# One attention layer on one core: where a last round's adds run, in which order its last pair comes, and when a gate-and-up tile uses its third weights again

## The chip, the cores and the metric

The kernel runs on one core of one Trainium2 chip. A core has TensorE (matrix products, into the eight banks of PSUM), VectorE, ScalarE, GpSimd (POOL on the profile's rows) and SyncE, which here only starts transfers. Each engine works through its own queue in order, and the engines wait for one another on semaphores. The metric is the device time of one execution in microseconds.

## The reference

One decoder layer over 512 tokens of width 1024, in f32: a feed-forward block (SwiGLU) before and one after a mixing block of windowed attention, a convolution module and attention to a memory. The change touches the two feed-forward blocks:

```python
def swiglu(x, w_gate, w_up, w_down):
    return (jax.nn.silu(x @ w_gate) * (x @ w_up)) @ w_down
...
x = x + 0.5 * swiglu(rms_norm(x, g_ffn1[l]), w_ffn1_gate[l], w_ffn1_up[l], w_ffn1_down[l])
...
x = x + 0.5 * swiglu(rms_norm(x, g_ffn2[l]), w_ffn2_gate[l], w_ffn2_up[l], w_ffn2_down[l])
```

The inner width is 2816, that is 22 tiles of 128.

## The kernel before

Everything is held transposed: features on the 128 partitions, tokens along the free dimension, so `x` is eight row blocks of 128 by 512. Precision comes from splitting each operand into a high and a low part (`fp32r`) and making three products for each block: high by high, high by low, low by high. For weights the class `Weights` does this: a load into a raw tile (`wraw`, four buffers, L178 on SyncE), sums of weights where a tile needs them (`make_sums`, L160 to L163, and `four`, L147 to L150, on VectorE), a cast on ScalarE (L214, L208) and the difference on VectorE (L219, L209). The split weights lie in four buffers in turn; one kind lies in a buffer of its own, `vhi` and `vlo`. `W.next()` hands out the next item and asks for the conversion of those three ahead.

**Gate and up tiles.** For most of the 22 tiles (`fast`, 18 in the first block and 19 in the second) gate and up are made together with seven half-width products in place of eight, after Strassen's way with sums of weights and of inputs. `product` issues one of them: twelve matmuls of 256 columns (L609 to L611). A tile has three banks: `b` and `c` of half width and `de` of full width. Its order is: first weights `w0` (B_11 into `b`, copied out by L620; B_21 into the left half of `de`), second `w1` (B_Q1 into the right half of `de`, copied out by L624; B_Q2 on top of `b`, copied out by L626), third `w2` (B_22 on top of the right half of `de`). L629 and L630 make `g` of that. Then comes the first part of a down step, if the tile has one; then `w3` (`vhi`, `vlo`), whose product B_T4 goes into `c` and is copied out by L638; then the second use of `w2`, B_T3, on top of `b`. L640 makes `u` from `c`'s copy and `b`, L644 multiplies it by `g`, and L567 and L568 split the result (`hh`, `hl`). The rest of the down step follows.

**Down steps.** `down` multiplies finished tiles of a round by down weights (`mm3`, L414 to L416) and adds half of the result to `x` (L671). Steps of one round are spread over the tiles of the next: most tiles carry one load with two steps, of 24 matmuls of 256 columns.

**The last round.** In the second block the last four tiles' down products are made in the same seven-product way. `paired` prepares the inputs (L472 to L492, seven blocks for each of two pairs of tiles), and `seven(g)` for g = 0 to 3 makes the row blocks 2g and 2g+1 of the output. `prod` issues six matmuls (L510 to L512). `half` copies a partial sum out with a factor (L515, ScalarE). `add` puts sums that several row blocks share into `x`: for g = 0 and 1 by an accumulating DMA on POOL (L521), for g = 2 and 3 by VectorE (L519). `leave` makes a row block of the output (L529, VectorE) and stores it (L532, SyncE). The leaves of g are put off into `seven(g+1)` by way of the list `later`; only g = 3 leaves its own, first block 6 whole, then the two halves of block 7. Pair g = 2 has the two banks `tp`, the other pairs two of the four banks `mm` each.

**What sets the order.** In the last round the program's own order holds on TensorE, VectorE and ScalarE (`tc.manual_schedule`). Everywhere else a planner in the language's framework orders each engine's queue, by the program's order and by when it reckons operands and buffers to be ready. Buffers and banks are handed on as soon as their last reader is done.

Of the kernel before, what the change touches and what calls it, by code (L numbers as in the profile page):

```python
# [39 lines left out]
T = 512  # L40
# [41 lines left out]
B_T3, B_Q1, B_Q2, B_T4, B_21, B_22, B_11 = range(7)  # L82
H_11, H_21, H_T1, H_T2, H_T4, H_T3, H_22 = range(7)
# [191 lines left out]
def layer(tc, ctx, a):  # L275
# [10 lines left out]
    def nm(s):  # L286
        uid[0] += 1
        return f"{s}_{uid[0]}"

    def mm_bank():  # L290
        return psum.tile([P, T], F32, tag="mm", name=nm("mm"), bufs=4)

    def sc_bank():
        return psum.tile([P, T], F32, tag="sc", name=nm("sc"), bufs=2)
# [4 lines left out]
    def work():  # L299
        return tmp.tile([P, T], F32, tag="t", name=nm("t"), bufs=5)  # L300
# [5 lines left out]
    W = Weights(nc, wpool, dma_ahead=3, conv_ahead=3, bufs=(4, 4))  # L306
# [51 lines left out]
    def atile(name, dtype=F32R):  # L358
        return act.tile([P, T], dtype, tag="h", name=nm(name), bufs=N_ACT)
# [68 lines left out]
    class Norm:  # L428
# [5 lines left out]
        def add(self, d, engine=POOL):  # L434
            sq = work() if d else tmp.tile([P, T], F32, tag="sqsum", name=nm("sqsum"), bufs=1)
            ACT.activation(sq, x[:, d], AF.Square)
            if d == 0:
                self.sum = sq
            else:
                (engine if d < KT - 1 else DVE).tensor_tensor(self.sum, self.sum, sq, op=ALU.add)  # L440
# [20 lines left out]
    def ffn(pool, norm, first, gain, hooks, next_gain, last):  # L461
# [35 lines left out]
        def seven(g):  # L497

            l, r = slice(0, 256), slice(256, 512)
            end = g == 3  # L500
            bank = tp_bank if g == 2 else mm_bank
            b, de, c = bank()[:, l], bank(), sc_bank()[:, l]
            s12, s45 = (kept(), work()) if end else (atile("s12", F32), atile("s45", F32))
            x0, x1 = x[:, 2 * g], x[:, 2 * g + 1]

            def prod(ps, w, at, step, block, first):
                for q in range(2):
                    hi, lo = sevens[q][block]
                    s = slice(at + q * step, at + q * step + P)
                    PE.matmul(ps, w[0][:, s], hi, start=first and q == 0, stop=False, skip_group_check=not first)  # L510
                    PE.matmul(ps, w[0][:, s], lo, start=False, stop=False, skip_group_check=not first)
                    PE.matmul(ps, w[1][:, s], hi, start=False, stop=q == 1, skip_group_check=not first)  # L512

            def half(to, ps, sign=1):
                ACT.activation(to, ps, AF.Copy, scale=0.5 * sign)  # L515

            def add(to, part):
                if g > 1:
                    DVE.tensor_tensor(to, to, part, op=ALU.add)  # L519
                else:  # L520
                    POOL.dma_start(to, part, accum_op=ALU.add)  # L521

            def leave(d, t, ps):
                o = work()[:, : t.stop - t.start]
                xd = x[:, d, t]
                if ps.shape[-1] < t.stop - t.start:
                    o, xd = (v.rearrange("p (a b) -> p a b", a=2) for v in (o, xd))
                    ps = ps.unsqueeze(1).to_broadcast([P, 2, 256])
                DVE.scalar_tensor_tensor(o, ps, 0.5, xd, op0=ALU.mult, op1=ALU.add)  # L529
                if len(o.shape) == 3:  # L530
                    o = o.rearrange("p a b -> p (a b)")
                nc.sync.dma_start(a["out"][d, :, t], o)  # L532

            W.split_to(W.at + 4)
            if g < 2:
                W.four(W.items[W.at + 4][0])
            wa, ws = W.next(), W.next()
            prod(b, wa, 0, 256, H_11, True)
            half(s12[:, l], b)
            prod(de[:, l], wa, 128, 256, H_21, True)  # L540
            prod(de[:, r], ws, 0, 128, H_T1, True)
            half(s45[:, r], de[:, r])
            while later:
                leave(*later.pop(0))
            prod(b, ws, 256, 128, H_T2, False)
            half(s12[:, r], b)
            add(x0, s12)
            prod(c, wa, 512, 128, H_T4, True)
            half(s45[:, l], c, -1)
            add(x1, s45)  # L550
            W.split_to(W.at + 3)
            prod(de[:, r], ws, 768, 128, H_22, False)
            prod(b, ws, 512, 128, H_T3, False)
            whole = slice(0, T)
            if end:
                leave(2 * g, whole, de)
                leave(2 * g + 1, l, b)
                leave(2 * g + 1, r, b)
            else:
                later.extend([(2 * g + 1, whole, b), (2 * g, whole, de)])  # L560

        def hidden(f, t):
            if plan.seven and f >= plan.rounds[-1][0]:
                paired(f, t)
                return
            h_hi[f], h_lo[f] = atile("hh"), atile("hl")
            ACT.copy(h_hi[f], t)  # L567
            DVE.tensor_tensor(h_lo[f], t, h_hi[f].bitcast(F32), op=ALU.subtract)  # L568

        def kept():  # L570
            return pool.tile([P, T], F32, tag="kept", name=nm("kept"), bufs=3)
# [32 lines left out]
        def product(ps, w, woff, block, first):  # L604
            wh, wl = w
            for k in range(4):
                c = slice(woff + k * P, woff + (k + 1) * P)
                one, end = first and k == 0, k == 3
                PE.matmul(ps, wh[:, c], bh[k][:, block], start=one, stop=False, skip_group_check=not first)  # L609
                PE.matmul(ps, wh[:, c], bl[k][:, block], start=False, stop=False, skip_group_check=not first)  # L610
                PE.matmul(ps, wl[:, c], bh[k][:, block], start=False, stop=end, skip_group_check=not first)  # L611

        def fast(f, mid):

            l, r = slice(0, 256), slice(256, 512)
            b, de, c = mm_bank()[:, l], mm_bank(), sc_bank()[:, l]
            s12, s45, g, u = kept(), kept(), work(), work()
            w0 = W.next()
            product(b, w0, 0, B_11, True)
            ACT.copy(s12[:, l], b)  # L620
            product(de[:, l], w0, 512, B_21, True)
            w1 = W.next()
            product(de[:, r], w1, 0, B_Q1, True)
            ACT.activation(s45[:, r], de[:, r], AF.Copy, scale=-1.0)  # L624
            product(b, w1, 512, B_Q2, False)
            ACT.copy(s12[:, r], b)  # L626
            w2 = W.next()
            product(de[:, r], w2, 0, B_22, False)
            DVE.tensor_tensor(g, de, s12, op=ALU.add)  # L629
            ACT.activation(g, g, AF.Silu)  # L630
            rest = []
            for d in mid:
                rest += down(*d)
            if rest:
                rest.pop(0)()
            w3 = W.next()
            product(c, w3, 0, B_T4, True)
            ACT.copy(s45[:, l], c)  # L638
            product(b, w2, 512, B_T3, False)
            DVE.tensor_tensor(  # L640
                u.rearrange("p (a b) -> p a b", a=2), s45.rearrange("p (a b) -> p a b", a=2),
                b.unsqueeze(1).to_broadcast([P, 2, 256]), op=ALU.subtract,
            )
            DVE.tensor_tensor(u, u, g, op=ALU.mult)  # L644
            hidden(f, u)
            for d in rest:
                d()
# [35 lines left out]
        for f in range(NF):  # L683
# [6 lines left out]
            else:  # L690
                g, u = (sc_bank(), sc_bank()) if f % 3 == 2 else (mm_bank(), mm_bank())
# [27 lines left out]
        r = plan.last  # L719
        if plan.seven:  # L720
            W.conv_ahead = -1
            with tc.manual_schedule(engines={mybir.EngineType.PE, mybir.EngineType.DVE, mybir.EngineType.Activation}):
                for g in range(4):
                    seven(g)
            return nxt
# [173 lines left out]
    load, piece, sums, p1, p2 = memory()  # L899
# [6 lines left out]
    with tc.tile_pool(name="fast1", bufs=1) as pool:  # L906
        norm = ffn(pool, norm, STARTS, C_G1, hooks, C_GM, False)
# [4 lines left out]
    with tc.tile_pool(name="fast2", bufs=1) as pool:  # L912
        ffn(pool, norm, [(0, 1, 2, 3, 4, 5, 6), (7,)], C_G2, {}, None, True)
# [490 lines left out]
```

## Time and profile before

| | us |
|---|---|
| runs of the kernel (three) | 861.43, 861.53, 861.96 |
| median | 861.53 |
| the profiled execution | 861.62 |
| its span in the profile | 859.8 |
| TensorE busy in it | 850.1 |
| VectorE busy | 708.9 |
| ScalarE busy | 466.3 |

The span is what the profile covers; the execution's own time has 1.82 us more around it. A row of the timeline gives the start, the duration, engine, line, operation, output and inputs by their names in the program, shapes, how many were merged, and in brackets the idle time before it and what ended that. A row with x2 is two instructions; the next may start a little before the one ahead has ended, so costs within a queue are best taken from start to start. "PE" is TensorE, "DVE" VectorE, "ACT" ScalarE. A waits row gives who waited on whom, then the sum, the number of times and the longest.

### The profile page before, as it was taken

The page shows a single profiled execution, that of the slowest core. Times are in us where ns is not written, and L with a number is a line of the kernel's source. Part 1 is how long each engine was busy: PE and PEld are TensorE (multiplying, and loading weights), DVE is VectorE, ACT ScalarE, POOL GpSimd, SP SyncE. Part 2 cuts the span into 40 slices and gives each one's busy share as a digit, 9 for nine tenths or more (in the row PEclk, how much of TensorE's full clock was granted, in tenths as well). Part 3 has the DMA queues.
Part 4 walks back from the last instruction along what each step waited for, and adds up shares of the span by engine and source line. Part 5 has one row for each costly group of instructions (what it writes and reads, how often), then busy time and mean ns, then how long its engine had stood idle before and what let it go on. Part 6 is the DMA issues. An engine that isn't in the chain of part 4 may idle for free. (4 is left out here: it accounts for less than half of the span.)

```text
span 859.8 us, 15853 instructions
## 1 busy us (share of the span) xinstructions
PE 850.1 (99%) x6397; PEld 788.6 (92%) x6397; DVE 708.9 (82%) x1208; ACT 466.3 (54%) x792; POOL 37.4 (4%) x40
## 2 busy tenths in 40 slices
PE   8999999999999999999999999999999999999997
PEld 5889999999999999988676788889999999999997
DVE  7998977877868897869989985899787878787896
ACT  7465555455654444633948764656554544545554
POOL 0000000000000000300000022120000000000001
PEclk9999999999999999999999999999999999999999
DMA  7335334333453434222010323863334342323325
GB/s 274 123 91 149 105 98 125 98 119 127 129 157 120 123 111 130 74 98 62 13 32 31 113 97 100 178 141 122 123 98 124 99 123 86 114 96 103 95 75 148
DMA packets 36795, 95.13 MB, mean 111 GB/s; under 512 B 3441, under 2 KB 8049, under 8 KB 36721
## 3 DMA queue, kind: packets, MB, share of 16 engines
q1 hardware_dynamic: 32032, 85.99, 32.1%
q0 software_dynamic: 3536, 6.55, 4.6%
q10 hardware_dynamic: 1152, 1.57, 0.6%
q8 instruction: 50, 0.82, 0.4%
q14 instruction: 25, 0.20, 0.1%
HBM read 88.07 MB, written 2.10 MB: 105 GB/s over the span
## 5 line engine op out<-in xcount | busy, mean ns | idle before, releaser
L609 PE MATMUL mm<-bh,w 128*128 128x256 f32 x888 | 245.5, 276 | 0.4 <-ACT kept L624 0.4
L610 PE MATMUL mm<-bl,w 128*128 128x256 f32 x888 | 245.2, 276 | 0.0
L611 PE MATMUL mm<-bh,w 128*128 128x256 f32 x888 | 245.2, 276 | 0.0
L609 PEld LDWEIGHTS mm<-bh,w 128*128 128x128 f32 x888 | 166.7, 188 | 0.8 <-ACT kept L624 0.6
L415 PE MATMUL mm<-hl,w 128*128 128x256 f32 (+1 forms) x584 | 167.3, 287 | 0.0
L416 PE MATMUL mm<-hh,w 128*128 128x256 f32 (+1 forms) x584 | 167.2, 287 | 0.0
L414 PE MATMUL mm<-hh,w 128*128 128x256 f32 (+1 forms) x584 | 167.0, 287 | 0.0
L610 PEld LDWEIGHTS mm<-bl,w 128*128 128x128 f32 x888 | 166.7, 188 | 0.1
L611 PEld LDWEIGHTS mm<-bh,w 128*128 128x128 f32 x888 | 166.7, 188 | 0.0
L214 ACT CAST w<-wraw 128x1024 fp32r<-128x1024 f32 (+2 forms) x119 | 119.1, 1005 | 74.8 <-PE mm L611 23.7
L219 DVE TENSOR_TENSOR w<-wraw,w 128x1024 fp32r<-128x1024 f32 (+2 forms) x113 | 132.5, 1176 | 29.9 <-ACT w L214 26.4
L219 DVE TENSOR_TENSOR w<-s,w 128x1024 fp32r<-128x1024 f32 x78 | 95.3, 1222 | 40.3 <-PE mm L611 34.5
L414 PEld LDWEIGHTS mm<-hh,w 128*128 128x128 f32 x584 | 109.6, 188 | 2.4 <-ACT hh L567 0.3
L415 PEld LDWEIGHTS mm<-hl,w 128*128 128x128 f32 x584 | 109.6, 188 | 2.2
L416 PEld LDWEIGHTS mm<-hh,w 128*128 128x128 f32 x584 | 109.6, 188 | 2.1
L214 ACT CAST w<-s 128x1024 fp32r<-128x1024 f32 x78 | 81.9, 1052 | 27.1 <-PE mm L611 20.4
L414 PE MATMUL mm<-xh,w 128*128 128x512 f32 x176 | 69.7, 401 | 0.5 <-ACT xh L425 0.4
L415 PE MATMUL mm<-xl,w 128*128 128x512 f32 x176 | 69.4, 394 | 0.6 <-DVE xl L426 0.5
L416 PE MATMUL mm<-xh,w 128*128 128x512 f32 x176 | 69.1, 393 | 0.0
L630 ACT ACTIVATE t<-t 128x512 f32<-128x512 f32 x37 | 23.4, 633 | 68.3 <-DVE t L629 68.3
L671 DVE SCALAR_TENSOR_TENSOR x<-mm,x 128x512 f32<-128x512 f32 x80 | 54.2, 683 | 2.0 <-PE mm L416 2.0
L214 ACT CAST vhi<-wraw 128x512 fp32r<-128x512 f32 x37 | 23.0, 621 | 42.7 <-PE sc L610 34.7
(290 smaller groups left out, 1496.8 us busy)
## 6 DMA issues: line engine op xcount, KB each, us to landing
wraw<-in_wgu SPq DMA_DIRECT2D x86, 512.0 KB, 3.6
wraw<-in_wd SPq DMA_DIRECT2D x38, 512.0 KB, 3.6
wraw<-in_win SPq DMA_DIRECT2D x12, 512.0 KB, 3.5
wraw<-in_wd SPq DMA_DIRECT2D x8, 384.0 KB, 3.3
x<-t POOLq DMA_DIRECT2D x8, 256.0 KB, 4.1
out<-t SPq DMA_DIRECT2D x7, 256.0 KB, 2.3
x<-in_xT SPq DMA_DIRECT2D x3, 512.0 KB, 6.8
wraw<-in_wout_a SPq DMA_DIRECT2D x6, 256.0 KB, 2.7
```

What stands on the lines that cost most here:

```text
L214: nc.scalar.copy(hi[:, :cols], raw[:, :cols])
L219: nc.vector.tensor_tensor(lo[:, :cols], raw[:, :cols], hi[:, :cols].bitcast(F32), op=ALU.subtract)
L414: PE.matmul(ps[:, t], wh[:, w], hi(k)[:, t], start=one, stop=False, skip_group_check=cut > 1)
L415: PE.matmul(ps[:, t], wh[:, w], lo(k)[:, t], start=False, stop=False, skip_group_check=cut > 1)
L416: PE.matmul(ps[:, t], wl[:, w], hi(k)[:, t], start=False, stop=end, skip_group_check=cut > 1)
L609: PE.matmul(ps, wh[:, c], bh[k][:, block], start=one, stop=False, skip_group_check=not first)
L610: PE.matmul(ps, wh[:, c], bl[k][:, block], start=False, stop=False, skip_group_check=not first)
L611: PE.matmul(ps, wl[:, c], bh[k][:, block], start=False, stop=end, skip_group_check=not first)
L630: ACT.activation(g, g, AF.Silu)
L671: DVE.scalar_tensor_tensor(o, ps, 0.5, xd, op0=ALU.mult, op1=ALU.add)
```

## The change

Three edits. First, in `seven` the limit for adds by VectorE goes from g > 1 to g > 0, so that g = 1 also adds with L519's instruction and no longer with a POOL DMA. Second, g = 3 has a third bank `e` for the product H_21, which before went to the left half of `de`, and another order of products: H_11, T1, T4, T2, H_21, T3, H_22 (before: H_11, H_21, T1, T2, T4, H_22, T3). Its leaves stand between them: the left half of block 6 behind H_21, the whole of block 7 behind T3, the right half of block 6 behind H_22. For g below 3 the order stays. Third, in `fast` the product B_T3 stands straight after `g`'s two instructions, ahead of the down step and of `w3`.

```diff
             def add(to, part):
-                if g > 1:
+                if g > 0:
                     DVE.tensor_tensor(to, to, part, op=ALU.add)
...
+            e = bank()[:, l] if end else de[:, l]
+
+            def p2():
+                prod(e, wa, 128, 256, H_21, True)
+
+            def p4():
+                prod(c, wa, 512, 128, H_T4, True)
+                half(s45[:, l], c, -1)
+                add(x1, s45)
+
+            def p3():
+                prod(de[:, r], ws, 768, 128, H_22, False)
+
+            def p7():
+                prod(b, ws, 512, 128, H_T3, False)
+
             prod(b, wa, 0, 256, H_11, True)
             half(s12[:, l], b)
-            prod(de[:, l], wa, 128, 256, H_21, True)
+            if not end:
+                p2()
             prod(de[:, r], ws, 0, 128, H_T1, True)
             half(s45[:, r], de[:, r])
             while later:
                 leave(*later.pop(0))
+            if end:
+                p4()
             prod(b, ws, 256, 128, H_T2, False)
             half(s12[:, r], b)
             add(x0, s12)
...
-            if end:
-                leave(2 * g, whole, de)
-                leave(2 * g + 1, l, b)
-                leave(2 * g + 1, r, b)
-            else:
+            if not end:
+                p4()
+                W.split_to(W.at + 3)
+                p3()
+                p7()
                 later.extend([(2 * g + 1, whole, b), (2 * g, whole, de)])
+                return
+            p2()
+            leave(2 * g, l, e)
+            p7()
+            leave(2 * g + 1, whole, b)
+            p3()
+            leave(2 * g, r, de[:, r])
...
             ACT.activation(g, g, AF.Silu)
+            product(b, w2, 512, B_T3, False)
             rest = []
...
             ACT.copy(s45[:, l], c)
-            product(b, w2, 512, B_T3, False)
```

More of the change, by code (lines that the diff above doesn't have):

```diff
@@ L537, in seven @@
             wa, ws = W.next(), W.next()
+            whole = slice(0, T)
+            e = bank()[:, l] if end else de[:, l]
[9 more added lines that the diff above has]
+                prod(b, ws, 512, 128, H_T3, False)
             prod(b, wa, 0, 256, H_11, True)
             half(s12[:, l], b)
-            prod(de[:, l], wa, 128, 256, H_21, True)
+            if not end:
+                p2()
             prod(de[:, r], ws, 0, 128, H_T1, True)
@@ L547, in seven @@
             add(x0, s12)
[L548 to L554, printed above, removed]
-            if end:
-                leave(2 * g, whole, de)
-                leave(2 * g + 1, l, b)
-                leave(2 * g + 1, r, b)
-            else:
-                later.extend([(2 * g + 1, whole, b), (2 * g, whole, de)])
+            if not end:
[3 more added lines that the diff above has]
+                p7()
+                later.extend([(2 * g + 1, whole, b), (2 * g, whole, de)])
+                return
[5 more added lines that the diff above has]
+            leave(2 * g, r, de[:, r])
         def hidden(f, t):
```

## The prediction

> **What bounds the kernel now.** I read the page's head first, then the busy times of one long stretch, then the timeline of the last 16 us engine by engine, and only then a single gate-and-up tile. The page and the stretch from 640 to 820 us (columns: length, then PE, PEld, DVE, ACT, POOL busy with instruction counts, granted clock, DMA share, GB/s):
>
> ```profile
> span 859.8 us, 15853 instructions
> PE 850.1 (99%) x6397; PEld 788.6 (92%) x6397; DVE 708.9 (82%) x1208; ACT 466.3 (54%) x792; POOL 37.4 (4%) x40
> 640.00:820.00 180.00, 180.00 (x1591) 180.00 (x1590) 141.86 (x191) 90.27 (x140) 0.00 (x0) 1.00 0.36 106
> ```
>
> TensorE is busy 180.00 of 180.00 us at a granted clock of 1.00: 180 / 1591 = 0.113 us for each matmul of 256 columns. The change removes no matmul. So it can gain in two places only: where TensorE waits, or after its last matmul. The rest of the work has to hide behind TensorE, and can only lose. The timelines of VectorE, TensorE and ScalarE in the last round:
>
> ```profile
> 844.42 1.28 DVE L529 SCALAR_TENSOR_TENSOR t<-mm,x 128x512 f32<-128x512 f32 x2
> 845.62 1.02 DVE L209 TENSOR_TENSOR w<-wraw,w 128x512 fp32r<-128x512 f32 x2
> 846.56 1.22 DVE L219 TENSOR_TENSOR w<-s,w 128x1024 fp32r<-128x1024 f32 x1
> 850.08 1.29 DVE L529 SCALAR_TENSOR_TENSOR t<-mm,x 128x512 f32<-128x512 f32 x2 [2.30 <-DMA x<-s]
> 851.28 1.28 DVE L519 TENSOR_TENSOR x<-x,s 128x512 f32<-128x512 f32 x2
> 852.66 1.29 DVE L529 SCALAR_TENSOR_TENSOR t<-tp,x 128x512 f32<-128x512 f32 x2
> 853.87 0.69 DVE L519 TENSOR_TENSOR x<-x,kept 128x512 f32<-128x512 f32 x1
> 854.47 0.69 DVE L519 TENSOR_TENSOR x<-x,t 128x512 f32<-128x512 f32 x1
> 855.07 1.35 DVE L529 SCALAR_TENSOR_TENSOR t<-mm,x 128x512 f32<-128x512 f32 x3
> ...
> 849.89 0.28 PE L510 MATMUL mm<-h,w 128*128 128x256 f32 x1
> 853.17 0.28 PE L512 MATMUL sc<-h,w 128*128 128x256 f32 x1
> 854.53 0.28 PE L512 MATMUL mm<-h,w 128*128 128x256 f32 x1
> ...
> 853.49 0.38 ACT L515 ACTIVATE t<-sc 128x256 f32<-128x256 f32 x1 [0.30 <-PE sc L512]
> ```
>
> The reader is to see that the last matmul starts at 854.53, and that VectorE goes on to 855.07 + 1.35 = 856.42. It is late because it stood still from 847.78 (846.56 + 1.22) to 850.08, waiting for the accumulating DMAs of g = 1, and has run without a pause of more than 0.1 us since. So **the end is VectorE's queue, not TensorE**. What follows its last instruction: SyncE's stores, and what the DMA engines moved (same columns as above).
>
> ```profile
> 855.78 1.30 SPq L532 DMA_DIRECT2D out<-t  x3
> ...
> 856.50:857.00 0.50, 0.00 (x0) 0.00 (x0) 0.00 (x0) 0.00 (x0) 0.00 (x0) 1.00 0.78 287
> 857.00:857.50 0.50, 0.00 (x0) 0.00 (x0) 0.00 (x0) 0.00 (x0) 0.00 (x0) 1.00 0.97 348
> 858.00:858.50 0.50, 0.00 (x0) 0.00 (x0) 0.00 (x0) 0.00 (x0) 0.00 (x0) 1.00 0.20 66
> ```
>
> The three last stores (512 KB) are issued one behind the other until 857.08, their data moves at 348 GB/s from about 856.6 to 858.1, and 1.7 us more pass to the end of the span.
>
> **Part 1: g = 1's two adds go from a POOL DMA to VectorE.**
>
> ```profile
> 843.96 1.74 POOL L521 DMA_DIRECT2D x<-s  x2 [3.02 <-DVE s L148]
> DVE t L529 <- DMA x<-s: 2.3, 1, 2.3
> DMA to landing us min/median/max: 3.3/3.8/5.4
> ```
>
> Removed: two POOL DMAs of 256 KB, and the 2.3 us wait. Added: two L519 adds of 512 columns. Two stand back to back at 853.87 and 854.47, so one costs 0.60 from start to start, 1.2 together. They come right behind the pair of L529 at 844.42. POOL took up the first at 843.96 and spent about 0.9 on each (1.74 / 2), so both inputs were there by 844.8, and the adds wait for nothing. From start to start the queue then reads: L529 twice 1.20 (to 845.62), adds 1.20 (846.82), L209 0.94 (847.76), L219 1.2 (848.9), L529 of g = 1 1.2 (850.1), adds of g = 2 1.2 (851.3), L529 of g = 2 1.2 (852.5). Before, that last pair ended at 853.87, so VectorE is ahead by 2.3 - 1.2, and some 0.2 of small gaps: about 1.3. Behind the adds are queued the L209 and L219 that finish the weights of g = 3. They end at 848.98; the first matmul that reads the L219's result comes 0.9 us into g = 3 (T1 is now its second product), at 849.89 + 0.68 + 0.23 = 850.80. Cover 1.8 us, cost nothing; without it the loss would be what the 1.2 us delay exceeds it by.
>
> The landing is where a rule speaks against this part. The Trainium skill, DMA: Bandwidth & Descriptors, section Anatomy of one DMA, gives such a transfer about 2.0 us plus its bytes over 436 GB/s; an estimate from it for 256 KB is 2.6 us, so the second accumulate, issued by 845.7, would land by 848.3, the wait would be 0.5, and VectorE would lose 0.7 by the swap. The trace does not agree: the wait lasted to 850.08, and the longest landing is 5.4 us.
>
> **Part 2: g = 3 reordered, with one PSUM bank more.** Seven products of six matmuls are left, 0.68 each from 849.89. The new order H_11, T1, T4, T2, H_21, T3, H_22 starts them at 849.89, 850.57, 851.25, 851.93, 852.61, 853.29, 853.97; TensorE's end does not move. A product's result is taken up 0.32 after its last matmul starts (853.17 to 853.49 above), and a ScalarE copy takes 0.38. T4's copy is done at 851.81 + 0.32 + 0.38 = 852.51, so x1's add runs 852.55 to 853.15; T2's copy is done at 853.19, so x0's add runs 853.2 to 853.8. Then the left half of row block 6 from its own bank (H_21 is done at 853.49): 128x256, 0.35, to 854.15. Then all of block 7 (T3 is done at 854.17): 0.6, to 854.8. Last the right half of block 6, which needs H_22: 854.53 + 0.32 = 854.85, and with 0.42 VectorE ends at **855.27, 1.15 before 856.42**. The extra bank is one of those that g = 1 held, freed at 850.1, 2.5 us before H_21 writes it: no wait. The number and sizes of stores are the same (one of 256 KB and two of 128 KB), but they are issued at 854.2, 854.8 and 855.3 as their data comes, while before the last issue stood behind two others and began about 0.3 after its data. Block 7's data starts 0.8 after its issue and takes 0.75, to 856.35; the last 128 KB follow in 0.38, to 856.75, against 858.1 before. The end gains between 1.15 (VectorE) and 1.4 (data); I take **1.3**.
>
> **Part 3: in 37 gate and up tiles B_T3 goes ahead of the down step, so B_T4 is now its tile's last product.** A tile of the steady stretch, by TensorE, ScalarE, VectorE:
>
> ```profile
> 710.49 0.28 PE L609 MATMUL sc<-bh,vhi 128*128 128x256 f32 x1
> 711.85 0.28 PE L609 MATMUL mm<-bh,w 128*128 128x256 f32 x1
> 713.09 0.28 PE L611 MATMUL mm<-bh,w 128*128 128x256 f32 x1
> 715.93 0.28 PE L609 MATMUL mm<-bh,w 128*128 128x256 f32 x1
> ...
> 711.98 0.62 ACT L214 CAST vhi<-wraw 128x512 fp32r<-128x512 f32 x1 [1.52 <-PE sc L610]
> 712.50 0.37 ACT L638 COPY kept<-sc 128x256 f32<-128x256 f32 x1
> 713.46 1.05 ACT L214 CAST w<-s 128x1024 fp32r<-128x1024 f32 x1 [0.59 <-PE mm L611]
> ...
> 713.49 0.68 DVE L640 TENSOR_TENSOR t<-kept,mm 128x512 f32<-128x512 f32 x1
> 714.82 1.22 DVE L219 TENSOR_TENSOR w<-s,w 128x1024 fp32r<-128x1024 f32 x1
> ```
>
> Moved earlier: T3 by a down step and a product, 4.1 us by the matmuls between (36 x 0.113), and with it the release of the third weights' buffer, on which the L214 at 713.46 waits. That conversion ends at 716.04 and is read 48 matmuls (5.4 us) into the next tile, at 721.4: it was already 5 us early, and earlier is worth nothing to TensorE. Moved later: T4 by 1.36 us (12 matmuls), so the vhi cast at 711.98, the copy L638 (712.50 to 713.86), and u in L640 (713.49 to about 714.27). The load that waits for vhi's source moves by 1.36 too, on SyncE; its weights are for the tile after next. L640 would end at 714.95, and the next tile begins at 715.93: 1.0 us of cover. I cost this part at **zero**. It is the unknown of the change, since the planner orders these instructions afresh and the trace does not show how. One stall can be gained, the only one in either stage that is clearly a wait:
>
> ```profile
> 615.82 0.28 PE L611 MATMUL mm<-bh,w 128*128 128x256 f32 x1
> 616.53 0.39 PE L609 MATMUL mm<-bh,w 128*128 128x256 f32 x1 [0.44 <-ACT kept L624]
> ...
> 615.58 0.62 ACT L567 CAST hh<-t 128x512 fp32r<-128x512 f32 x1 [1.07 <-DVE t L644]
> 616.10 0.38 ACT L624 ACTIVATE kept<-mm 128x256 f32<-128x256 f32 x1
> ```
>
> From 615.82 to 616.53 are 0.6 us more than the pitch of 0.113: the next product wants L624's copy, queued behind a cast that waits for VectorE. Another order can remove it, or repeat it. So the ends of part 3 are -0.6 and the slow rival's price below, and I take zero, the value of the steady rows.
>
> **Sum.** The profiled execution took 861.62, 1.82 more than its span; the median of the runs is 861.53, 0.09 less. 861.53 - 1.3 + 0 = **860.2**, which is 0.15% less. About 0.2% (1.7 us) is what a measurement of this kernel can tell from no change.
>
> **The rivals.** *A: part 3 removes the 0.6 us stall as well*: 859.6. For it: T3's earlier release gives VectorE work in its waits for DMA. Against: VectorE is the late engine there, and its work is the same.
>
> *B: the tail gives less, because the wait moved.* In the new g = 3 VectorE's pieces (0.6, 0.6, 0.35, 0.6, 0.42) fill 852.5 to 855.27 but for 0.2 us. Whatever is late by more adds to the end: a hand-over of 0.1 us at each of five pieces, or stores that queue as they did before. That takes half the gain: 860.9.
>
> *C, the slow one: u comes too late for the next tile's bank.* If the next tile's first product takes the bank that L640 reads, it waits for L640. The third weights' L219 is now ready ahead of L640; if the planner puts it there, L640 starts 1.13 us later. Two tiles have no room:
>
> ```profile
> 127.89 0.68 DVE L640 TENSOR_TENSOR t<-kept,mm 128x512 f32<-128x512 f32 x1
> 128.59 0.28 PE L609 MATMUL mm<-bh,w 128*128 128x256 f32 x1
> ...
> 625.36 0.68 DVE L640 TENSOR_TENSOR t<-kept,mm 128x512 f32<-128x512 f32 x1
> 626.17 0.28 PE L609 MATMUL mm<-bh,w 128*128 128x256 f32 x1
> ```
>
> They lose 1.1 and 1.0, which gives 862.3. In a steady tile L640 would end at 714.95 + 1.13 = 716.08, 0.15 too late; over the other 26 tiles with a down step that is 3.9 more, 866.2. It decides from 1.3 us on. Against it: L219 could as well go ahead of the copy L638, where it delays nothing.
>
> **How the numbers follow.** Forecast 860.2: 0.47. A: 0.25. B: 0.16. C: 0.12. The range runs from 859.3, just under A, to 862.3, C's lower price; about 0.15 lies outside. Faster by over 0.2% (under 859.8) is most of A and an edge of the forecast: 0.27. Slower by over 0.2% (over 863.25) is the larger half of C: 0.07. Within: 0.66.
>
> **What would show it.** Right: no DMA wait ahead of L529; VectorE's last instruction a 128x256 L529 that starts 0.3 after the last matmul and ends some 1.15 nearer to it; the span's end closer to the last matmul by 1.3; from 640 to 820 still 180 us of PE. Wrong: a gap on TensorE ahead of a tile's first L609, released by L640 (C); a last L529 more than 0.5 after TensorE's end (B); L624 no longer releasing L609 near 616 (A).

## The result, and the profile after

The changed kernel takes **866.65 us** (median of 6 runs, 865.73 to 868.55), the kernel before 861.77 beside it (6 runs). The ratio is 1.0057, with a 95% interval of 1.0044 to 1.0070: 4.9 us slower, where 1.3 us faster was forecast and the range ended at 862.3. In the changed code the lines of the gate and up tiles stand 20 further down: the matmuls L609 to L611 are L629 to L631, the copies L620, L624 and L626 are L640, L644 and L646, the silu L630 is L650, `u` (L640) is **L660**, its product with `g` (L644) is **L664**, the cast `hh` (L567) is **L587**. The copy of T4 (L638) is L659, and a down step's L671 is L691.

The profiled execution took 866.61. Its page, at the head and in the costliest group, with the same group of before below it:

```profile
span 864.8 us, 15799 instructions
...
...
L629 PE MATMUL mm<-bh,w 128*128 128x256 f32 x888 | 246.7, 278 | 3.3 <-ACT kept L644 1.6
```

```profile
L609 PE MATMUL mm<-bh,w 128*128 128x256 f32 x888 | 245.5, 276 | 0.4 <-ACT kept L624 0.4
```

The last column is TensorE's idle time ahead of these matmuls. It went from 0.4 to 3.3 us, and ScalarE's copies ended most of it. The waits of the changed kernel say the same in full, and show others that have grown; those of before follow:

```profile
ACT hh L587 <- DVE t L664: 78.7, 31, 4.4
...
DVE s L160 <- DMA wraw<-in_wgu: 35.8, 26, 2.6
...
PE mm L629 <- ACT kept L644: 1.6, 4, 0.6
PE mm L629 <- ACT kept L640: 1.5, 3, 0.9
```

```profile
ACT hh L567 <- DVE t L644: 25.9, 28, 2.2
...
DVE s L160 <- DMA wraw<-in_wgu: 23.2, 24, 2.2
```

The reader is to see that the first fence has seven waits of TensorE for copies, where before had one (L609 on L624, 0.4, quoted above); that the cast `hh` waits 78.7 us for its input in place of 25.9; and that VectorE's first sum of weights (L160) waits 12.6 us longer for its loads (the section on the loads shows how little the last total says).

**The tail came out as forecast.** VectorE and TensorE in the last round of the changed kernel:

```profile
851.70 1.28 DVE L519 TENSOR_TENSOR x<-x,s 128x512 f32<-128x512 f32 x2
852.90 1.02 DVE L209 TENSOR_TENSOR w<-wraw,w 128x512 fp32r<-128x512 f32 x2
...
860.13 1.35 DVE L529 SCALAR_TENSOR_TENSOR t<-mm,x 128x256 f32<-128x256 f32 x3
...
860.72 0.28 PE L512 MATMUL mm<-h,w 128*128 128x256 f32 x1
```

The two new adds run from 851.70 to 852.90, 1.2 us from start to start, and no L529 waits for a DMA any more. VectorE ends at 860.13 + 1.35 = 861.48, that is 0.76 after the start of the last matmul, where before it was 856.42 - 854.53 = 1.89. From the last matmul's start to the end of the span it is 864.8 - 860.72 = 4.08, before 859.8 - 854.53 = 5.27. So the tail gained **1.19**.

**The loss is ahead of it.** The last matmul starts at 860.72 in place of 854.53, 6.2 us later. Stretches of the gate and up tiles show where it came from (columns as in the windows above: length, PE, PEld, DVE, ACT, POOL, granted clock, DMA share, GB/s). After, then before:

```profile
640.00:820.00 180.00, 179.87 (x1587) 179.67 (x1586) 142.57 (x192) 86.28 (x139) 0.00 (x0) 1.00 0.34 105
175.00:245.00 70.00, 68.49 (x596) 67.72 (x595) 55.96 (x75) 36.69 (x62) 1.71 (x2) 1.00 0.45 133
585.00:625.00 40.00, 38.59 (x333) 37.81 (x332) 36.44 (x49) 22.82 (x40) 0.00 (x0) 1.00 0.38 124
```

```profile
175.00:245.00 70.00, 70.00 (x620) 70.00 (x620) 53.10 (x72) 37.73 (x62) 1.71 (x2) 1.00 0.43 129
585.00:625.00 40.00, 39.56 (x349) 39.37 (x348) 35.64 (x50) 22.90 (x38) 0.00 (x0) 1.00 0.38 118
```

In the first block's stretch TensorE issued 596 matmuls in place of 620, 24 x 0.113 = 2.7 us less work in the same time. In the second block's first tiles it is 333 for 349, 1.8 us. The long steady stretch lost next to nothing. At a granted clock of 1.00 in all of them it isn't the clock. The rest lies at the start of the mixing block (L415 waits on L426 for 1.3 in all, 0.5 before) and in pieces of 0.5 or less. The waits for copies lie in the same two stretches: all three of 1.5 on L640 between 175 and 245 us, three of the four on L644 between 585 and 625.

**How one tile loses.** The tile that starts at 204.41 lost the most. TensorE, ScalarE and VectorE:

```profile
204.41 0.28 PE L629 MATMUL mm<-bh,w 128*128 128x256 f32 x1
...
208.38 0.28 PE L631 MATMUL mm<-bh,w 128*128 128x256 f32 x1
209.57 0.38 PE L629 MATMUL mm<-bh,w 128*128 128x256 f32 x1 [0.92 <-ACT kept L640]
...
206.89 0.62 ACT L587 CAST hh<-t 128x512 fp32r<-128x512 f32 x1 [2.99 <-DVE t L664]
207.42 1.05 ACT L214 CAST w<-wraw 128x1024 fp32r<-128x1024 f32 x1
208.37 0.90 ACT L789 ACTIVATE mh<-t,par 128x256 fp32r<-128x256 f32 x2
209.17 0.35 ACT L640 COPY kept<-mm 128x256 f32<-128x256 f32 x1
...
200.70 0.69 DVE L160 TENSOR_TENSOR s<-wraw 128x512 f32<-128x512 f32 x1 [2.43 <-DMA wraw<-in_wgu]
...
201.91 1.22 DVE L219 TENSOR_TENSOR w<-s,w 128x1024 fp32r<-128x1024 f32 x1
...
205.45 0.68 DVE L660 TENSOR_TENSOR t<-kept,mm 128x512 f32<-128x512 f32 x1
```

Read it from the wait backwards. The tile's fourth product, B_Q2, writes over `b`, so it needs the copy L640 of B_11, which TensorE had finished long before: the last of B_11's twelve matmuls starts 11 x 0.113 = 1.25 us after 204.41. But on ScalarE the copy stands behind `hh` of the *previous* tile, a conversion and two activations. `hh` was late because VectorE started `u` only at 205.45, more than 1 us into the tile; before, `u` started 1.76 ahead of this tile. VectorE ran without a pause from L160 to `u`, so the 2.80 us are two terms: L160 had waited 2.43 for a load and started 3.71 ahead of the tile in place of 5.38 (1.67), and the third weights' L219 (1.13 from start to start) had been put ahead of `u`. ScalarE took its queue in order: it stood idle for 2.99 ahead of `hh`, with the conversion and the copy behind it.

### The profile page after: what moved, and what is told of

It reads as the page before. It is cut to its first block, busy times and chain, and to the rows that moved or that the text cites. A ratio compares the mean times of both kernels' runs of the same rounds, so it can differ in the third digit from the quotient of the medians.

```text
span 864.8 us, 15799 instructions
## 1 busy us (share of the span) xinstructions
PE 852.1 (99%) x6397; PEld 789.2 (91%) x6397; DVE 715.3 (83%) x1210; ACT 458.1 (53%) x792; POOL 35.5 (4%) x38
## 5 line engine op out<-in xcount | busy, mean ns | idle before, releaser
L629 PE MATMUL mm<-bh,w 128*128 128x256 f32 x888 | 246.7, 278 | 3.3 <-ACT kept L644 1.6
L630 PE MATMUL mm<-bl,w 128*128 128x256 f32 x888 | 245.3, 276 | 0.0
L631 PE MATMUL mm<-bh,w 128*128 128x256 f32 x888 | 245.3, 276 | 0.0
L629 PEld LDWEIGHTS mm<-bh,w 128*128 128x128 f32 x888 | 166.7, 188 | 5.4 <-ACT kept L644 3.0
L415 PE MATMUL mm<-hl,w 128*128 128x256 f32 (+1 forms) x584 | 167.2, 287 | 0.0
L414 PE MATMUL mm<-hh,w 128*128 128x256 f32 (+1 forms) x584 | 167.1, 287 | 0.1
L630 PEld LDWEIGHTS mm<-bl,w 128*128 128x128 f32 x888 | 166.7, 188 | 0.1
L631 PEld LDWEIGHTS mm<-bh,w 128*128 128x128 f32 x888 | 166.7, 188 | 0.0
L219 DVE TENSOR_TENSOR w<-wraw,w 128x1024 fp32r<-128x1024 f32 (+2 forms) x113 | 133.0, 1178 | 22.2 <-ACT w L214 18.2
L214 ACT CAST w<-wraw 128x1024 fp32r<-128x1024 f32 (+2 forms) x119 | 119.0, 1004 | 59.1 <-issue 30.7
L219 DVE TENSOR_TENSOR w<-s,w 128x1024 fp32r<-128x1024 f32 x78 | 95.4, 1222 | 37.1 <-PE mm L631 28.0
L414 PEld LDWEIGHTS mm<-hh,w 128*128 128x128 f32 x584 | 109.5, 188 | 2.8 <-ACT hh L587 0.8
L415 PEld LDWEIGHTS mm<-hl,w 128*128 128x128 f32 x584 | 109.6, 188 | 2.3 <-DVE hl L588 0.2
L214 ACT CAST w<-s 128x1024 fp32r<-128x1024 f32 x78 | 81.9, 1051 | 47.8 <-PE mm L631 40.8
L414 PE MATMUL mm<-xh,w 128*128 128x512 f32 x176 | 69.6, 400 | 1.2 <-ACT w L230 1.2
L415 PE MATMUL mm<-xl,w 128*128 128x512 f32 x176 | 69.5, 395 | 1.4 <-DVE xl L426 1.3
L587 ACT CAST hh<-t 128x512 fp32r<-128x512 f32 x33 | 20.5, 622 | 78.7 <-DVE t L664 78.7
L214 ACT CAST vhi<-wraw 128x512 fp32r<-128x512 f32 x37 | 23.0, 621 | 66.1 <-issue 55.5
L691 DVE SCALAR_TENSOR_TENSOR x<-mm,x 128x512 f32<-128x512 f32 x80 | 54.5, 684 | 1.3 <-PE mm L416 0.9
```

What stands on the lines that cost most here:

```text
L214: nc.scalar.copy(hi[:, :cols], raw[:, :cols])
L219: nc.vector.tensor_tensor(lo[:, :cols], raw[:, :cols], hi[:, :cols].bitcast(F32), op=ALU.subtract)
L414: PE.matmul(ps[:, t], wh[:, w], hi(k)[:, t], start=one, stop=False, skip_group_check=cut > 1)
L415: PE.matmul(ps[:, t], wh[:, w], lo(k)[:, t], start=False, stop=False, skip_group_check=cut > 1)
```

## The experiments

Two theories stood at the start. The **queue theory**: `u` comes late, `hh` holds up ScalarE's queue, and the next tile's copies and conversions come late with it. The **bank theory** (rival C): the next tile's matmuls wait for VectorE to read the bank. Both allow the L219 ahead of `u` as the first cause; a third possibility was that the last round's edits cost something ahead of the tail.

### The two halves of the change

First the last round's edits alone (parts 1 and 2): `B_T3` goes back to its old place.

```diff
             ACT.activation(g, g, AF.Silu)
-            product(b, w2, 512, B_T3, False)
             rest = []
...
             ACT.copy(s45[:, l], c)
+            product(b, w2, 512, B_T3, False)
```

> Parts 1 and 2 alone; B_T3 stands in its old place. Every theory that puts the loss into part 3 expects the forecast of the last round: the end comes 1.2 us nearer to the last matmul and nothing else moves, 860.4 us against some 861.6 of the kernel before (0.14% less). A rival, that the last round's own changes (the POOL transfers gone, another length of the program) shift the planner's order elsewhere, expects TensorE to wait in the gate and up tiles here too and a time over 862.

Then part 3 alone, on the kernel before:

```diff
             ACT.activation(g, g, AF.Silu)
+            product(b, w2, 512, B_T3, False)
             rest = []
...
             ACT.copy(s45[:, l], c)
-            product(b, w2, 512, B_T3, False)
```

> Part 3 alone; the last round is that of the kernel before. If the loss is all part 3, the time is that of the changed kernel plus the last round's 1.2 us: about 867.8. If the parts meet (for example because the last round starts late and hides its gain), it is the changed kernel's 866.6 or less.

Measured: parts 1 and 2 alone 861.03 against 862.39, ratio 0.9985 (0.9976 to 0.9994), 1.4 us faster. Part 3 alone 867.45, ratio 1.0057 (1.0040 to 1.0075), 5.1 us slower. The whole loss is part 3's, and the tail's gain is real; the two ratios multiplied give 1.0042, beside 1.0057 (1.0044 to 1.0070) for the change.

### Which of part 3's instructions does it

Third weights' difference behind `u`: VectorE keeps the L219 of the moved item back until `u` is issued.

```diff
+            W.conv_ahead = 2
             w3 = W.next()
+            W.conv_ahead = 3
...
-            DVE.tensor_tensor(
+            made = DVE.tensor_tensor(
                 u.rearrange("p (a b) -> p a b", a=2), s45.rearrange("p (a b) -> p a b", a=2),
                 b.unsqueeze(1).to_broadcast([P, 2, 256]), op=ALU.subtract,
             )
+            with tc.issue_after(made.ins):
+                W.split_to(W.at + 3)
```

> The changed kernel, but the third weights' conversion is asked for behind u, and VectorE's part of it (L219) is held behind the instruction that makes u, as it stood before. Order theory (what costs is that this 1.13 us instruction now stands ahead of u, so that the cast of the tile's result, and ScalarE's copies behind it, come late): most of the waits in tiles with a down step vanish, some 2.5 us of 4.5, and the time falls to about 863.5. Chain theory (it is B_T4 as the tile's last product that brings u, the cast and the copies behind it late, whatever else VectorE does): under 1 us is won, 866 or more.

Measured: 862.81, ratio 1.0003 (0.9994 to 1.0012). That is 4.6 of the 4.9 us that the change lost. The stretch of the first block is full again, and two waits of 0.3 for the copies are left. A tile of this kernel's steady stretch, VectorE, ScalarE and TensorE:

```profile
717.49 0.68 DVE L662 TENSOR_TENSOR t<-kept,mm 128x512 f32<-128x512 f32 x1
718.09 1.22 DVE L219 TENSOR_TENSOR w<-s,w 128x1024 fp32r<-128x1024 f32 x1
719.22 0.69 DVE L668 TENSOR_TENSOR t<-t,t 128x512 f32<-128x512 f32 x1
...
719.06 1.05 ACT L214 CAST w<-wraw 128x1024 fp32r<-128x1024 f32 x1 [1.94 <-issue]
720.01 0.61 ACT L587 CAST hh<-t 128x512 fp32r<-128x512 f32 x1
...
718.82 0.28 PE L629 MATMUL mm<-bh,w 128*128 128x256 f32 x1
```

Time came back as the order theory expected, but not by its path. The next tile's first matmul starts at 718.82, so `hh` starts 1.19 behind it, no earlier than in the changed kernel (1.01 in a steady tile, worked out below). `u` is ahead of L219 now, but its product with `g` (L668), which the cast needs, is still behind it. In the stretch that is full again `hh` starts 1.3 to 2.2 behind. What did change ahead of the copies is ScalarE's order, by the planner's answer: the conversion L214 runs ahead of `hh`, while `hh` waits, and no longer between `hh` and the copy of B_11. So this run doesn't show that L219 ahead of `u` is what costs.

Cast behind the copies: L219 stays where the change put it, and `hh` and `hl` are issued behind the next tile's copy of B_Q1.

```diff
+        held_back = []
...
-            ACT.activation(s45[:, r], de[:, r], AF.Copy, scale=-1.0)
+            copied = ACT.activation(s45[:, r], de[:, r], AF.Copy, scale=-1.0)
+            with tc.issue_after(copied.ins):
+                while held_back:
+                    hidden(*held_back.pop(0))
...
-            hidden(f, u)
+            held_back.append((f, u))
...
                 fast(f, mid)
+                while f == NF - 1 and held_back:
+                    hidden(*held_back.pop(0))
```

> The changed kernel, but ScalarE's cast of a tile's result is held behind the next tile's copy of B_Q1, so that it can no longer stand ahead of the copies L640 and L644 that TensorE waits for. Queue theory (TensorE waits because the copies stand behind a cast that waits for VectorE; chain and order theory both run through this queue): the waits of L629 on ScalarE fall from some 5.5 us to under 1, and the time to about 861. Bank theory (the next tile's first product waits for the bank that u reads): nothing changes, 866.6.

Measured: 861.00, ratio 0.9983 (0.9974 to 0.9991). Its first block's stretch, a steady tile on ScalarE (L642 and L646 are the copies of B_11 and B_Q1 here), VectorE and TensorE, and its waits for the loads:

```profile
175.00:245.00 70.00, 70.00 (x620) 70.00 (x620) 56.54 (x75) 38.97 (x64) 1.71 (x2) 1.00 0.45 130
```

```profile
717.22 0.37 ACT L642 COPY kept<-mm 128x256 f32<-128x256 f32 x1 [0.27 <-PE mm L631]
...
720.00 0.39 ACT L646 ACTIVATE kept<-mm 128x256 f32<-128x256 f32 x1 [0.33 <-PE mm L631]
720.28 0.61 ACT L587 CAST hh<-t 128x512 fp32r<-128x512 f32 x1
...
710.66 1.22 DVE L219 TENSOR_TENSOR w<-s,w 128x1024 fp32r<-128x1024 f32 x1
...
714.33 0.68 DVE L665 TENSOR_TENSOR t<-kept,mm 128x512 f32<-128x512 f32 x1
...
715.66 0.28 PE L629 MATMUL mm<-bh,w 128*128 128x256 f32 x1
```

```profile
DVE s L160 <- DMA wraw<-in_wgu: 13.9, 14, 1.9
```

L219 still runs ahead of `u` (L665), yet both copies follow their products within 0.33, and TensorE waits for no copy at all: 620 matmuls as before. `hh` itself is later than in the runs above, 4.62 behind the tile's first matmul (715.66), and TensorE doesn't wait for it. So the queue theory holds: what costs is the cast's place ahead of the copies on ScalarE. The **bank theory** expected no change. That it missed doesn't settle it, since `u` starts 1.33 ahead of the next tile here (2.44 before) and ends in time. It **falls by the changed kernel's own trace**: near 204 `u` reads its bank from 205.45 on, 1.04 after the next tile's first matmul, and nothing had held that matmul. That the waits for loads fell from 35.8 to 13.9 as well, although the edit touches no load, points to a loop, which a later run takes up.

Both products ahead: the first down step, too, goes behind B_T4, so that `u` is ready a down step earlier.

```diff
-            if rest:
-                rest.pop(0)()
             w3 = W.next()
+            if rest:
+                product(b, w2, 512, B_T3, False)
             product(c, w3, 0, B_T4, True)
             ACT.copy(s45[:, l], c)
+            if not rest:
+                product(b, w2, 512, B_T3, False)
```

> The changed kernel, but in tiles with a down step both B_T3 and B_T4 stand ahead of the step, so that u can be made a down step earlier; tiles without one keep the old order, T4 and then T3. Chain and order theory (u late, by T4 as last product and by L219 ahead of it) both expect no more waits in tiles with a down step: 861 or less, near 860.5. A rival, that it is the early release of the third weights as such that disturbs the planner (loads and conversions at other times), expects half the loss or more to stay: over 863.

Measured: 862.75 against 862.06, ratio 1.0007 (0.9998 to 1.0015). The mechanism came out as expected: the first block's stretch is full (620 matmuls), and one wait on a copy is left (0.5). The time did not: 0.7 over the kernel before, not 1.6 under it. In its profile L415 waits 1.1 us for L426, 0.5 before, and a low clock in the mixing block (last section) falls in that one execution. Two things bear on all eleven runs. Each took 2.06 to 2.16 us more than its span, against 1.72 to 1.87 in the other runs of the experiments, so some 0.3 lies outside the span. And only four had a mean granted clock of 0.999 or more; their median is 861.55, beside 861.66 of the ten such runs of the kernel before. So the clock accounts for the 0.7, as far as four runs can show it, but not for what is missing to the expected 860.5; that is open.

### The loop through the loads

A steady tile shows how lateness carries over. The changed kernel, ScalarE, VectorE and TensorE, and the loads that SyncE starts; then the same tile before:

```profile
716.38 0.69 DVE L160 TENSOR_TENSOR s<-wraw 128x512 f32<-128x512 f32 x1 [0.95 <-DMA wraw<-in_wgu]
...
717.59 1.22 DVE L219 TENSOR_TENSOR w<-s,w 128x1024 fp32r<-128x1024 f32 x1
718.73 0.69 DVE L161 TENSOR_TENSOR s<-wraw,s 128x512 f32<-128x512 f32 x1
...
721.13 0.68 DVE L660 TENSOR_TENSOR t<-kept,mm 128x512 f32<-128x512 f32 x1
...
721.56 0.28 PE L629 MATMUL mm<-bh,w 128*128 128x256 f32 x1
...
719.50 0.36 ACT L659 COPY kept<-sc 128x256 f32<-128x256 f32 x1
722.57 0.62 ACT L587 CAST hh<-t 128x512 fp32r<-128x512 f32 x1 [2.71 <-DVE t L664]
...
725.42 1.77 SPq L178 DMA_DIRECT2D wraw<-in_wgu  x2
```

```profile
709.87 0.69 DVE L160 TENSOR_TENSOR s<-wraw 128x512 f32<-128x512 f32 x1
...
714.93 0.62 ACT L567 CAST hh<-t 128x512 fp32r<-128x512 f32 x1 [0.42 <-DVE t L644]
...
718.51 3.05 SPq L178 DMA_DIRECT2D wraw<-in_wgu  x2
```

Against the start of the next tile's first matmul (721.56, before 715.93), `hh` moved from 1.0 ahead to 1.0 behind, 2.0 us in all. Two terms make that up. L219 ahead of `u` is 717.59 to 718.73, 1.14. L160 starts 5.18 ahead of the tile in place of 6.06, 0.88. The copy of B_11 moved along by 0.9 (from 1.56 to 2.49 behind the start of its tile), which is harmless here and not where two activations more stand in the queue (above). The conversion behind `hh` frees a raw tile for the next load. So the pair of loads starts 3.86 into the tile in place of 2.58, and its issues take 1.77 together in place of 3.05, so they lie closer together. That is how a late `hh` could make the next L160 late, and with it the next `hh`. It is a reading so far; the next run takes out one link.

The totals of L160's waits have to be split by stretch before they say anything. From 640 to 820 they do follow the change: 2.8 us before, 11.5 with the change, 1.8 with parts 1 and 2 alone. But that stretch lost next to nothing. From 175 to 245, where most was lost, they are 4.0 before and 7.8 with the change, but 8.4 with parts 1 and 2 alone and 9.1 in a run of part 2 alone (below), where TensorE issued 619 and 617 matmuls of 620. So late loads alone cost next to nothing there (0.1 and 0.3 us), and they aren't a mark of part 3. With parts 1 and 2 alone `hh` starts up to 1.3 behind its tile in this stretch without loss; in the change it starts 1.5 to 2.7 behind.

One conversion first: `hh` is issued only behind the conversion that `W.next()` asks for, but ahead of the copies.

```diff
-                nc.scalar.copy(hi[:, :cols], raw[:, :cols])
+                self.last_cast = nc.scalar.copy(hi[:, :cols], raw[:, :cols])
...
+        held_back = []
...
             w0 = W.next()
+            with tc.issue_after(W.last_cast.ins):
+                while held_back:
+                    hidden(*held_back.pop(0))
...
-            hidden(f, u)
+            held_back.append((f, u))
...
                 fast(f, mid)
+                while f == NF - 1 and held_back:
+                    hidden(*held_back.pop(0))
```

> The changed kernel, but ScalarE's cast of a tile's result is held behind one weight conversion of the next tile (the first L214), which so far stood right behind it. The cast still stands ahead of both copies, and L219 still ahead of u. Loop theory (the late cast holds up that conversion, so the next gate weights' buffer comes free late, the two loads follow each other closely and land late, VectorE's sums wait for them, and u and the cast come late again): VectorE's waits for gate and up loads fall from 35.8 us to under 25, and the time to about 863 or less. If the loads do not matter, and only the cast's place ahead of the copies does: 866 to 867.

Measured: 863.83 against 862.31, ratio 1.0016 (1.0008 to 1.0025). Its waits for the loads:

```profile
DVE s L160 <- DMA wraw<-in_wgu: 14.0, 11, 2.6
```

The waits for loads fall from 35.8 to 14.0 by the order of ScalarE's instructions alone, with L219 still ahead of `u`, and 3.5 of the 4.9 us come back. So the link of the loop on ScalarE is shown: the cast's place there changes how long VectorE waits for loads. That the time came back by way of the loads isn't shown, because the same edit also takes a conversion of 1.05 us out from between `hh` and the copy of B_11. The three waits for that copy are gone, and the four for the copy of B_Q1 (1.6) remain. This run has a wait of its own, too: 1.2 of TensorE (L414) for a cast `hh` near 562, at the start of the second block. That the two loads hinder one another when close together was not tried by itself.

Third and fourth swapped: B_T3 goes behind the first down step, but ahead of B_T4. T4 is then as late as in the change, while the third weights are let go later.

```diff
             ACT.activation(g, g, AF.Silu)
-            product(b, w2, 512, B_T3, False)
...
             w3 = W.next()
+            product(b, w2, 512, B_T3, False)
             product(c, w3, 0, B_T4, True)
```

> The changed kernel, but B_T3 stays behind the first down step and only changes places with B_T4: the third weights come free 1.4 us earlier than in the kernel before, not 4.1, and B_T4 is still the tile's last product; the planner still puts L219 ahead of u. If what costs is the planner's order around a late B_T4, this is as slow as the changed kernel, 865 to 867. If it is the release 4.1 us earlier, it is 861 to 862.

Measured: 864.43 against 862.31, ratio 1.0021 (1.0011 to 1.0030), between the two cases of the expectation. B_T4 as its tile's last product costs 0.0036 over parts 1 and 2 alone (0.9985), 3.1 us, and B_T3 ahead of the down step as much again to 1.0057 (each ratio with an interval of about 0.001 to either side). VectorE again has L219 ahead of `u` (203.52 and 205.26 in the tile near 204), and the waits for loads add up to 33.5. How much of either is the planner's answer, and how much the move itself, stays open.

### The tail, one edit at a time

The kernel before with part 1 alone:

```diff
-                if g > 1:
+                if g > 0:
```

> Part 1 alone. By the forecast's steps VectorE is 1.3 us ahead when it comes to g = 3, but with the old order both adds and all leaves follow the fourth and fifth product: from the last matmul's start to VectorE's end it should be 1.35 us (1.89 in the kernel before, 0.76 in the changed one), so about half of the gain. If the wait for the DMA had been hidden anyway: 1.9.

And part 2 alone, that is the first kernel of the experiments (parts 1 and 2) with the limit set back:

```diff
-                if g > 0:
+                if g > 1:
```

> Part 2 alone, with the POOL transfers for g = 1. VectorE is then late by its wait and has the same work, so it runs back to back to the end: 1.9 us from the last matmul's start to VectorE's end, no gain. If the order alone were what matters: 0.8 to 1.0.

Each ran once (861.25 and 863.79), too little to rank them by time; what counts is the end of their profiles. VectorE and TensorE, with the adds alone and then with the order alone:

```profile
854.72 1.35 DVE L529 SCALAR_TENSOR_TENSOR t<-mm,x 128x512 f32<-128x512 f32 x3
...
854.74 0.28 PE L512 MATMUL mm<-h,w 128*128 128x256 f32 x1
```

```profile
852.14 1.29 DVE L529 SCALAR_TENSOR_TENSOR t<-mm,x 128x512 f32<-128x512 f32 x2 [2.29 <-DMA x<-s]
...
857.30 1.35 DVE L529 SCALAR_TENSOR_TENSOR t<-mm,x 128x256 f32<-128x256 f32 x3
...
856.71 0.28 PE L512 MATMUL mm<-h,w 128*128 128x256 f32 x1
```

From the last matmul's start to VectorE's end it is 856.07 - 854.74 = 1.33 with the adds alone, 858.65 - 856.71 = 1.94 with the order alone, 1.89 before and 0.76 with both. So the order is worth nothing while the 2.29 wait for the accumulating DMA stands ahead of it, the adds alone are worth 0.56, and together they are worth 1.13. The order pays only together with the adds.

### A version that beats both

The last round's edits, B_T3 in its old place, and the cast held behind the next tile's copy of B_Q1 (on parts 1 and 2 alone):

```diff
+        held_back = []
...
-            ACT.activation(s45[:, r], de[:, r], AF.Copy, scale=-1.0)
+            copied = ACT.activation(s45[:, r], de[:, r], AF.Copy, scale=-1.0)
+            with tc.issue_after(copied.ins):
+                while held_back:
+                    hidden(*held_back.pop(0))
...
-            hidden(f, u)
+            held_back.append((f, u))
...
                 fast(f, mid)
+                while f == NF - 1 and held_back:
+                    hidden(*held_back.pop(0))
```

> Parts 1 and 2, B_T3 in its old place, and the cast held behind the next tile's copy of B_Q1, as in the fourth run. If the one wait of the kernel before near 616 us is the same queue, it goes too: the last round's 1.2 and some 0.6, 0.2% under the kernel before. If the queue only matters where u is late, it is the first run's 0.15%.

Measured: **859.75** against 862.06, ratio 0.9970 (0.9961 to 0.9980), 2.3 us faster than the kernel before. TensorE waits for no copy in any tile, the stall near 616 of the kernel before among them.

| kernel | ratio to before | 95% |
|---|---|---|
| the change | 1.0057 | 1.0044 to 1.0070 |
| parts 1 and 2 | 0.9985 | 0.9976 to 0.9994 |
| part 3 | 1.0057 | 1.0040 to 1.0075 |
| change, difference behind `u` | 1.0003 | 0.9994 to 1.0012 |
| change, cast behind copies | 0.9983 | 0.9974 to 0.9991 |
| change, both products ahead | 1.0007 | 0.9998 to 1.0015 |
| change, one conversion first | 1.0016 | 1.0008 to 1.0025 |
| change, B_T3 behind the down step | 1.0021 | 1.0011 to 1.0030 |
| parts 1 and 2, cast behind copies | 0.9970 | 0.9961 to 0.9980 |

## Why the prediction was wrong

**Parts 1 and 2 were right, term by term.** The adds were forecast at 1.2 and took 1.2. VectorE's end was forecast 0.74 after the last matmul's start and came at 0.76; with the adds alone it came at 1.33, beside the 1.35 that was expected of that run. The tail's gain was forecast at 1.3 and measured at 1.19 in the trace and 1.4 in the time of parts 1 and 2 alone. The rule from the Trainium skill (DMA: Bandwidth & Descriptors, section Anatomy of one DMA), by which the swap would have cost VectorE 0.7, did not decide: with the order alone the accumulating DMA held VectorE for 2.29 again, and the adds alone brought its end 0.56 nearer. Rival B, the wait that moves, did not come.

**The step that failed is part 3: "I cost this part at zero".** It rested on "L640 would end at 714.95, and the next tile begins at 715.93: 1.0 us of cover". Two things in it were wrong. The delay was reckoned as T4's 1.36 us, on the way through its copy; measured, that copy is done at 719.50 + 0.36 = 719.86 and `u` starts at 721.13, so T4 wasn't what `u` waited for. In its place came the L219 ahead of `u` (1.14) and the later L160 (0.88; 1.13 and 1.67 in the tile that lost most). And the cover was reckoned to the wrong reader. A late `u` was measured against the bank that the next tile needs. The cast `hh` behind it stands in ScalarE's queue ahead of the next tile's copies and conversions, and those have less room where other work stands there too: the first block's stretch lost 2.7 us, the steady one next to none.

**Rival C had the right instruction and the wrong path.** It put the L219 ahead of `u` at 1.13 (measured 1.14), but let it act through the bank: a gap ahead of a tile's first matmul, released by `u`. There is no such wait in the trace; the gaps stand ahead of the fourth and fifth products and are released by the copies. That its higher price, 866.2, lies by the measured 866.65 is chance: it was summed at 0.15 over 26 tiles, most of them steady, and the steady stretch from 640 to 820 lost 0.45 in all (1587 matmuls for 1591). Its argument against itself, that L219 could go ahead of the copy L638, "where it delays nothing", is what the planner did: L219 runs at 717.59, ahead of that copy (L659 now, 719.50). It delayed `u` all the same, because VectorE had no pause between L160 (716.38) and `u` (721.13).

**Part 3 said of the stall near 616 that another order "can remove it, or repeat it".** Where one wait of that kind stood there are seven, and no price stood for that; rival A priced only the removal. That was the term missing from the sum: the 0.6 us stall was an example of the mechanism, a copy behind a cast that waits for VectorE, and the prediction read it as an accident of one tile.

Still open: why both products ahead does not reach the time of parts 1 and 2 alone; how much of the cast's lateness costs by way of L219, of T4 and of the loads, since no run moved one of them alone; and what share of part 3's loss is the planner's reordering and what the move itself. A second buffer for `vhi` and `vlo`, which would free the conversion from T4, was not tried.

## What to carry to other kernels

A stall that occurs once shows what the schedule is short of: ask how many more such stalls a later operand makes, not only whether this one goes. For a result that comes later, follow every instruction behind it in its consumers' queues (here the cast, then the copies that let TensorE go on), not only the bank or buffer that it frees. Where a planner orders the queues, tie the waiting instruction behind the urgent ones by hand: on the better tail the ratio went from 0.9985 to 0.9970 by that alone, about 1.3 us, with intervals that just overlap.

## What was not expected of the hardware

The granted clock isn't the same in each execution. In three profiles (difference behind `u`, both products ahead, order alone) TensorE ran at 0.92 to 0.93 over 440 to 460 us, in the mixing block, and at 1.00 in the nine others. The row of both products ahead, with TensorE busy throughout and 0.92 in the column of the granted clock:

```profile
440.00:460.00 20.00, 20.00 (x115) 15.60 (x115) 17.96 (x91) 12.97 (x39) 0.20 (x1) 0.92 0.14 41
```

Eight per cent of 20 us is 1.6 us, an estimate of what it cost that execution, and more than the tail's whole gain; so single executions can't rank these kernels, and the ratios above stand on 10 or 11 runs each, 6 for the change and for part 3.
